# A hybrid encoder layer: half of the tokens normed before their transposes, two GLU tiles side by side, the gate tile first, and the first pair's weight sums on VectorE

## The chip, the cores and the metric

The kernel runs on one core of a Trainium2 chip. The metric is the device time of one execution in microseconds; where runs are repeated, the median is given. All times below are in microseconds unless they are marked as nanoseconds.

The names of the engines in the profile: PE is TensorE (matrix products, and transposes made as products with an identity), PEld its weight loads, DVE is VectorE, ACT is ScalarE, POOL is GpSimd, and SP is SyncE, which issues most of the DMAs. POOL issues those DMAs that add to what lies at their destination.

## The reference

One encoder layer over 1024 tokens of width 1024, all in float32. What is computed, cut to the part that the change touches:

```python
h = _rmsnorm(x, attn_norm_w)                 # x * rsqrt(mean(x*x) + EPS) * w
proj = h @ w_in                              # 1024 -> 8192 columns
glu_in, q, v, z_f, z_b, og, g_a, g_b = split(proj)
a = glu(glu_in)                              # first half * sigmoid(second half), 512 columns
a = dwconv_centred(a, 31 taps) -> layernorm -> silu -> @ pw_w
o = bidirectional HGRN2 scan of q, v, z_f, z_b, normed per head and gated by og
x = x + (sigmoid(g_a) * a + sigmoid(g_b) * o @ o_w) @ w_out
x = x + conv-gated feed-forward of rmsnorm(x)     # d_ff = 2816
return _rmsnorm(x, final_norm_w)
```

## The kernel before, in words

Activations are held transposed: a tile has 128 features on the partitions and 512 tokens along the row, so 1024 tokens are two halves and 1024 features are eight k tiles. Float32 products are made of three products with rounded operands: each operand is split into a high part (a cast on ScalarE, line 121) and a low part (source minus high part, line 118, on VectorE or GpSimd), and `mm3` (lines 143 to 145) issues high x high, high x low and low x high. One output tile of 128 columns for one half of the tokens is 8 k tiles x 3 = 24 products in one PSUM bank.

The order of TensorE's instructions is the order of the program text; the other engines' orders are made by a planner, which takes the text's order as priority and starts ahead of its turn what its cost model holds to be ready. Each engine then works strictly in its own order.

`Stream` and `run_jobs` interleave: a job is a preparation (load the raw weights into a "wr" buffer, of which there are two; split them into two "wp" pages, of which there are four) and a run that yields after every two k tiles (six products, a piece). `s_glu.fill(n)` puts n pieces into the text. When a job starts, the preparation of the next one is put into the text.

The stages around the change:

1. `load_x(0)` issues the loads of the first four tiles of x (128 tokens each), then `load_vectors` issues ten small loads of norm weights, biases and taps; `s_glu.fill()` issues the loads of the first two GLU weight tiles, and `load_x(1)` the other four tiles of x.
2. `input_norm(0)` handles the first half: ScalarE sums the squares of each token tile (line 436), TensorE transposes x itself, six of the eight k tiles ahead; GpSimd raises the mean to the power -1/2 (lines 404 and 405); `spread` brings this row statistic across the partitions with four scaled identities on ScalarE (line 411), a product with ones and a copy (lines 412 and 413). Then for each k tile VectorE multiplies the bank by the norm weight and by the spread statistic (line 455) into an "ev" page, ScalarE makes the high and GpSimd the low part, ScalarE copies the bare transposed x (line 457), and the normed tile and the copy are stored to `d_h` and `d_xt`.
3. The eight GLU column tiles (value j, then gate j, for j from 0 to 3) are made for the first half of the tokens, then again for the second half: 16 jobs of 24 products, 64 pieces. The value's bank is held until the gate's sigmoid (line 493) is there; VectorE's product (line 494) then frees both. `input_norm(1)` runs between these pieces, two pieces for each step.
4. `h_combos` (lines 292 and 508) loads normed tiles back from `d_h` and makes the sums of activations that Strassen's scheme needs; line 532 makes one more set. The remaining GLU pieces run beside it and `s_glu.drain()` ends the GLU.
5. `pair_job` makes two column tiles for both halves by seven instead of eight products of blocks (12 x 7 products, in the order 1, 2, 6, 7, 5, 4, 3). Its preparation needs sums of weight blocks, made by DMAs that add (line 238): `col += src1` from HBM, then the two halves of `rows` in turn. 17 such pairs follow, and the steps of the depthwise conv on VectorE (lines 642 and 645) are put between their pieces.

Behind this come the layer norm and pointwise product of the conv branch, the scans, and the rest of the layer. `x2_evac` loads `d_xt` back there for the residual sum.

The lines that set the pace in the text:

```python
s_glu = Stream(run_jobs([*glu_jobs(0), *glu_jobs(1)], prime=2))
norm0, norm1 = input_norm(0), input_norm(1)
next(norm0)
s_glu.fill()
load_x(1)
turn_vectors()
for _ in norm0:
    pass
s_glu.fill(GLU_FIRST)          # 4
for _ in norm1:
    s_glu.fill(GLU_FILL)       # 2
s_glu.fill(GLU_MORE)           # 16
```

## Time and profile before

| what | value |
|---|---|
| median of 3 runs | 1885.06 us (1883.33 to 1894.11) |
| the profiled execution | 1885.96 us |
| its span | 1884.2 us, 23705 instructions |
| granted TensorE clock, mean | 0.983 |
| ScalarE begins on the first x tile, on the fourth | 4.08 us, 8.70 us |
| first GLU product on TensorE | 21.60 us |
| first product of the first pair | 135.37 us |
| last product of the sixth set of the first pair | 160.22 us |
| last step of the depthwise conv on VectorE | 349.4 us |

How to read it. A row of the timeline has the start, the duration, the engine, the line of the kernel, the operation, its output and inputs by tile name, the shape, and in brackets how long the engine had stood idle and what released it. A row of a table by stretches has the stretch and its length, then the busy time and number of instructions of each engine, the granted TensorE clock (1.00 is full speed), the share of time in which the 16 DMA engines were busy, and what they moved. A row of the waits has who waited for whom, the total, how often, and the longest. Matrix products are pipelined: each is shown some 0.39 us long, but their starts are what counts.

### The profile page before, as it was taken

How to read it: one execution, taken by the hardware profiler on the slowest of the kernel's cores; microseconds unless marked ns; L12 is line 12 of the kernel's file. 1: busy time of each engine (PE TensorE's matmuls, PEld its weight loads, DVE VectorE, ACT ScalarE, POOL GpSimd, SP SyncE). 2: the span in 40 equal slices, each digit the busy share in tenths (PEclk: the TensorE clock that was granted, in tenths of full speed). 3: DMA queues.
4: the chain of work that ended last, by engine and by line, in shares of the span. 5: the costliest groups of instructions: out<-in, count | busy, mean ns of one | idle time of the engine just before them, and what ended most of it. 6: DMA issues, size and time to landing. Idle time of an engine off the chain costs nothing.

```text
span 1884.2 us, 23705 instructions
## 1 busy us (share of the span) xinstructions
PE 1790.5 (95%) x8543; PEld 1478.6 (78%) x8543; DVE 1270.1 (67%) x1860; ACT 797.2 (42%) x1488; POOL 198.0 (11%) x202
## 2 busy tenths in 40 slices
PE   6988999999999999999989999899999999999996
PEld 4767877877787888888878778688888788788885
DVE  3488999635459999989935556676666767534445
ACT  6333343324554655555442144543443434522124
POOL 3101112213100000000000000111111111000000
PEclk9999999999999999999999999999999999999998
DMA  7747788876572333322228666777676766633134
GB/s 264 222 116 165 181 183 204 188 177 156 176 224 79 118 96 117 109 91 93 84 90 240 194 193 185 165 164 145 145 160 147 154 140 129 216 97 94 55 92 162
DMA packets 322764, 282.99 MB, mean 150 GB/s; under 512 B 14798, under 2 KB 244950, under 8 KB 322646
## 3 DMA queue, kind: packets, MB, share of 16 engines
q1 hardware_dynamic: 270854, 240.57, 41.2%
q0 software_dynamic: 51792, 40.90, 15.6%
q8 instruction: 67, 1.10, 0.2%
q14 instruction: 51, 0.42, 0.1%
HBM read 189.14 MB, written 71.83 MB: 139 GB/s over the span
## 4 chain that ended last, share of the span: by engine, by line
PE 48%; DVE 21%; DMA 18%; ACT 6%; issue 4%; POOL 2%; SPq 0%; ACTq 0%; DVEq 0%; POOLq 0%
PE mm L143 12%; PE mm L144 12%; PE mm L145 12%; DMA wr<-wr 3%; DMA tm<-d_a 3%; DVE wp L118 2%; DMA wr<-sw 2%; PE sc L143 2%; PE sc L145 2%; PE sc L144 2%; DVE kG L730 2%; DMA sw<-in_w_in_dram 2%; DVE acc L645 2%; DMA wr<-in_w_in_dram 2%; DVE qF L730 2%
## 5 line engine op out<-in xcount | busy, mean ns | idle before, releaser
L143 PE MATMUL mm<-hx,wp 128*128 128x512 f32 x1176 | 481.4, 409 | 19.4 <-ACT su L266 5.1
L145 PE MATMUL mm<-hx,wp 128*128 128x512 f32 x1176 | 467.2, 397 | 4.3 <-DVE wp L118 4.3
L144 PE MATMUL mm<-hx,wp 128*128 128x512 f32 x1176 | 466.1, 396 | 2.4 <-POOL hx L118 2.4
L121 ACT CAST wp<-wr 128x1024 fp32r<-128x1024 f32 (+2 forms) x196 | 179.7, 917 | 341.8 <-PE mm L144 207.9
L118 DVE TENSOR_TENSOR wp<-wr,wp 128x1024 fp32r<-128x1024 f32 (+2 forms) x196 | 207.2, 1057 | 118.7 <-ACT wp L121 113.0
L143 PEld LDWEIGHTS mm<-hx,wp 128*128 128x128 f32 x1176 | 225.7, 192 | 69.5 <-ACT su L266 7.2
L145 PEld LDWEIGHTS mm<-hx,wp 128*128 128x128 f32 x1176 | 224.8, 191 | 55.6 <-DVE wp L118 6.7
L144 PEld LDWEIGHTS mm<-hx,wp 128*128 128x128 f32 x1176 | 225.6, 192 | 47.9 <-POOL hx L118 4.7
L645 DVE SCALAR_TENSOR_TENSOR acc<-gl,v_b,acc 128x1024 f32<-128x1024 f32 x120 | 149.3, 1279 | 0.5
L1259 DVE TENSOR_TENSOR xr<-mm,xr 128x512 f32<-128x512 f32 x48 | 33.2, 691 | 80.9 <-PE mm L145 80.9
L238 POOL DMA_DIRECT2D wr<-sw x39 | 34.6, 888 | 491.1 <-DVE wp L118 227.6
L838 PE MATMUL sc<-qF,A 128*128 128x128 f32 x512 | 68.8, 277 | 13.8 <-DVE qF L730 13.2
L838 PEld LDWEIGHTS sc<-qF,A 128*128 128x128 f32 x512 | 64.3, 192 | 21.1 <-issue 17.0
L121 ACT CAST wq<-sw 128x1024 fp32r<-128x1024 f32 x39 | 41.0, 1052 | 78.2 <-PE mm L144 68.5
L835 ACT COPY A<-kG 128x512 f32<-128x512 f32 x64 | 39.6, 618 | 73.3 <-DVE kG L730 50.8
L143 PE MATMUL mm<-hy,wp 128*128 128x512 f32 x156 | 62.3, 399 | 6.7 <-ACT wp L121 5.2
L1181 DVE SCALAR_TENSOR_TENSOR tm<-gp,v_a,tm 128x512 f32<-128x512 f32 x88 | 65.7, 748 | 2.3 <-ACT tm L1177 1.1
L266 ACT COPY su<-mm 128x512 f32<-128x512 f32 x78 | 45.3, 581 | 49.9 <-PE mm L145 49.7
L144 PE MATMUL mm<-hy,wp 128*128 128x512 f32 x156 | 62.1, 398 | 0.0
L145 PE MATMUL mm<-hy,wp 128*128 128x512 f32 x156 | 61.7, 396 | 0.0
L143 PE MATMUL sc<-hy,wq 128*128 128x512 f32 x156 | 61.3, 393 | 0.0
L143 PE MATMUL tr<-hx,wp 128*128 128x512 f32 x156 | 61.3, 393 | 0.0
(289 smaller groups left out, 3587.7 us busy)
## 6 DMA issues: line engine op xcount, KB each, us to landing
wr<-in_w_in_dram SPq DMA_DIRECT2D x55, 512.0 KB, 5.3
sw<-in_ffn_w_up_dram SPq DMA_DIRECT2D x44, 256.0 KB, 3.6
sw<-in_ffn_w_up_dram POOLq DMA_DIRECT2D x22, 512.0 KB, 8.9
wr<-in_ffn_w_up_dram SPq DMA_DIRECT2D x22, 512.0 KB, 5.2
d_g<-ft SPq DMA_DIRECT2D x44, 256.0 KB, 5.6
ev<-d_g SPq DMA_DIRECT2D x44, 256.0 KB, 2.8
wr<-sw POOLq DMA_DIRECT2D x39, 256.0 KB, 3.3
wr<-wr POOLq DMA_DIRECT2D x39, 256.0 KB, 4.4
```

The costliest lines, as they stand in the source:

```text
L118: eng.tensor_tensor(lo, src, hi.bitcast(F32), op=ALU.subtract)
L121: A.copy(hi, src)
L143: T.matmul(acc, whi[:, k, :], ahi, start=first, stop=False, skip_group_check=again)
L144: T.matmul(acc, whi[:, k, :], alo, start=False, stop=False, skip_group_check=again)
L145: T.matmul(acc, wlo[:, k, :], ahi, start=False, stop=last, skip_group_check=again)
L238: G.dma_start(o, a, accum_op=ALU.add)
L266: A.copy(t, acc)
L645: V.scalar_tensor_tensor(acc, g[:, k : k + S], tap(k), acc, op0=ALU.mult, op1=ALU.add)
L730: V.tensor_tensor(o, a, b, op=op)
L835: A.copy(A_t.rearrange("p (b x e) -> p b x e", x=2, e=h), pairs(kG, h))
L838: T.matmul(b[:, c * P : (c + 1) * P].rearrange("p (b x e) -> p b x e", x=2, e=h), A_t[:, c * P : (c + 1) * P], view(qF, c * P, [[2 * h, P ...
L1181: V.scalar_tensor_tensor(c, g[:, o + k : o + k + H], vec("fdw", k * NF + j), c, op0=ALU.mult, op1=ALU.add,)
```

## The change

It rewrites the prologue up to the first pair:

- The first half of the tokens is normed before its transposes. `first_norm` multiplies each token tile, 128 tokens on the partitions, by its own statistic (a scalar for each partition; VectorE, 128x1024), and TensorE transposes the result. So `spread` is not called for this half. From the bank ScalarE makes the high part with the norm weight as scale, VectorE the low part straight from the bank, and ScalarE a plain copy for the store to `d_h`. The bare x, which the residual sum needs, is transposed on its own, in eight groups of four transposes (`residual`), copied by VectorE and stored to `d_x0`, a layout in which four k tiles of one token tile lie together; `x2_evac` loads it back in pieces of 128 tokens.
- Only the norm weight's vector is loaded at the beginning; the other nine small loads and their transposes come after `second_norm` (which is the former `input_norm(1)`).
- The first two GLU tiles, gate 0 and value 0, run side by side: for each k tile three products of each (`glu_first`). The next three raw weight tiles are loaded early.
- The gate tile comes ahead of the value tile everywhere: its sigmoid goes into a "tm" page (`gate`), its bank is free then, and the value's product takes the page. The third tile is made for both halves at once; tiles 0, 1 and 2 of the second half follow, and the conv begins with tile 3.
- The first pair's weight sums are made by VectorE (`first=True`), with the second block's raw weights loaded into the second "wr" buffer, and its preparation is put into the text after 17 pieces beside `h_combos`, before the GLU ends. The other pairs keep the DMAs that add.

The diff, cut to its core (`store`, `todo` and `in_pair` are only moved up, and `in_pair` passes `first=n == 0`):

```diff
...
-GLU_MORE = 16
+GLU_MORE = 4
+GLU_LATE = 17
...
-    def pair_job(src0, src1, nk, acts, wpool, pool, evac, su=4):
+    def pair_job(src0, src1, nk, acts, wpool, pool, evac, su=4, first=False):
...
             def add(o, a):
-                G.dma_start(o, a, accum_op=ALU.add)
+                if first:
+                    V.tensor_tensor(o, o, a, op=ALU.add)
+                else:
+                    G.dma_start(o, a, accum_op=ALU.add)
 
...
-            add(col, src1)
+            add(col, raw_w(src1, 2 * nk) if first else src1)
...
@@ -337,12 +341,13 @@
         rows_in.append((v, r, n))
         return v
 
-    def turn_vectors():
-        b = bank("ob")
+    def turn_vectors(tag="ob"):
+        b = bank(tag)
         for i, (v, r, n) in enumerate(rows_in):
             T.transpose(b[:, i * P : i * P + n], r[:n, :], ident[:n, :n])
         for i, (v, r, n) in enumerate(rows_in):
             V.tensor_copy(v, b[:, i * P : i * P + n])
+        rows_in.clear()
...
-    v_a = load_vectors(
-        "v_a",
-        [
-            ("attn", rview(attn_norm_w), ND),
+    vecs = {"v_n": load_vectors("v_n", [("attn", rview(attn_norm_w), ND)])}
+    others = {
+        "v_a": [
...
-    )
-    v_b = load_vectors("v_b", [("cdw", rview(conv_dw_w), CK * NCW)])
-    v_c = load_vectors("v_c", [("fdb", rview(ffn_dw_b), NF)])
-    vecs = {"v_a": v_a, "v_b": v_b, "v_c": v_c}
+        "v_b": [("cdw", rview(conv_dw_w), CK * NCW)],
+        "v_c": [("fdb", rview(ffn_dw_b), NF)],
+    }
...
-    d_xt = scratch("d_xt", ND, 2)
+    d_x0 = dp.tile([P, 4, ND, P], F32, name="d_x0")
+    d_xt = [[d_x0[:, :, k, :], scratch(f"d_xt_{k}")] for k in range(ND)]
...
-    tags0 = iter(["sc", "tr", "sc", "tr", "mm", "mm", "sc", "tr"])
-
-    def input_norm(half):
-        xs = x_in[half * 4 : half * 4 + 4]
+    def first_norm():
+
+
+        xs = x_in[:4]
         ss = cp.tile([P, 4], F32, name=nm("ss"), tag="ss", bufs=2)
+        rs = cp.tile([P, 4], F32, name=nm("rs4"), tag="rs4", bufs=1)
+        xn = []
         for i, xt in enumerate(xs):
-            junk = p0.tile([P, D], F32, tag="junk", name=nm("junk"), bufs=2)
+            t = p0.tile([P, D], F32, tag="xn", name=nm("xn"), bufs=4)
+            A.activation(t, xt, AF.Square, accum_out=ss[:, i : i + 1])
+            rstd_small(rs[:, i : i + 1], ss[:, i : i + 1], D)
+            V.tensor_scalar(t, xt, rs[:, i : i + 1], None, op0=ALU.mult)
+            xn.append(t)
+
+        def residual(i, g, tag):
+            b = bank(tag)
+            for k in range(4):
+                T.transpose(
+                    b[:, k * P : (k + 1) * P], xs[i][:, (4 * g + k) * P : (4 * g + k + 1) * P], ident
+                )
+            t = page(p0, "xr", 7)
+            V.tensor_copy(t, b)
+            nc.sync.dma_start(
+                d_x0[:, i, 4 * g : 4 * g + 4, :], t.rearrange("p (k t) -> p k t", k=4)
+            )
+
+        def turn(b, i, k):
+            T.transpose(b[:, i * P : (i + 1) * P], xn[i][:, k * P : (k + 1) * P], ident)
+
+        residual(0, 0, "mm")
+        residual(0, 1, "mm")
+        turn_vectors("mm")
+        banks = [bank(t) for t in ("sc", "tr", "sc", "tr", "ob")]
+        for i in range(4):
+            for k, b in enumerate(banks):
+                turn(b, i, k)
+        yield
+        late = {2: (1, 0, "mm"), 3: (1, 1, "tr"), 4: (2, 0, "ob")}
+        late |= {5: (2, 1, "sc"), 6: (3, 0, "tr"), 7: (3, 1, "sc")}
+        for k in range(ND):
+            b, g = banks[k], vec("attn", k)
+            hi, lo, raw = hx(), hx(), page(p0, "raw", ND)
+            A.activation(hi, b, AF.Copy, scale=g)
+            V.scalar_tensor_tensor(lo, b, g, hi.bitcast(F32), op0=ALU.mult, op1=ALU.subtract)
+            A.activation(raw, b, AF.Copy, scale=g)
+            nc.sync.dma_start(d_h[k][0], raw)
+            ht[1 if k < NK2 else 2].append((hi, lo))
+            yield
+            if k + 5 < ND:
+                b = bank(("sc", "tr", "sc")[k])
+                for i in range(4):
+                    turn(b, i, k + 5)
+                banks.append(b)
+            if k in late:
+                residual(*late[k])
+
+    def second_norm():
+        xs = x_in[4:]
+        ss = cp.tile([P, 4], F32, name=nm("ss"), tag="ss", bufs=2)
+        junk = p0.tile([P, D], F32, tag="xn", name=nm("junk"), bufs=4)
+        for i, xt in enumerate(xs):
             A.activation(junk, xt, AF.Square, accum_out=ss[:, i : i + 1])
         banks = []
 
         def turn(k):
-            b = bank(next(tags0) if half == 0 else "tr")
+            b = bank("tr")
             for i in range(4):
                 T.transpose(b[:, i * P : (i + 1) * P], xs[i][:, k * P : (k + 1) * P], ident)
             banks.append(b)
 
-        ahead = 6 if half == 0 else 1
-        for k in range(ahead):
-            turn(k)
+        turn(0)
         yield
         rstd_small(ss, ss, D)
-        rs = spread(ss, bank("ob"), page(p0, "rs", 2))
+        rs = spread(ss, bank("ob"), page(p0, "rs", 1))
         yield
         for k in range(ND):
             b = banks[k]
@@ -455,13 +511,11 @@
             V.scalar_tensor_tensor(raw, b, vec("attn", k), rs, op0=ALU.mult, op1=ALU.mult)
             hl = split(hx(), hx(), raw, G)
             A.copy(xt, b)
-            if k + ahead < ND:
-                turn(k + ahead)
-            nc.sync.dma_start(d_h[k][half], raw)
-            nc.sync.dma_start(d_xt[k][half], xt)
-            if half == 0:
-                ht[1 if k < NK2 else 2].append(hl)
-            elif k < NK2:
+            if k + 1 < ND:
+                turn(k + 1)
+            nc.sync.dma_start(d_h[k][1], raw)
+            nc.sync.dma_start(d_xt[k][1], xt)
+            if k < NK2:
                 h12.append(hl)
             else:
                 ht[3].append(hl)
@@ -480,23 +534,117 @@
         G.memset(g[:, PAD + S :], 0.0)
         gl.append(g)
 
-    held = {}
-
-    def glu_jobs(half):
-        for j in range(NCW):
-
-            def evac_a(hf, acc):
-                held[0] = acc
-
-            def evac_b(hf, acc, j=j):
-                sg = tmp()
-                A.activation(sg, acc, AF.Sigmoid)
-                V.tensor_tensor(
-                    gl[j][:, PAD + hf * H : PAD + (hf + 1) * H], held[0], sg, op=ALU.mult
-                )
-
-            yield std_job(in_cols(j * P), ND, h_std, evac_a, (half,))
-            yield std_job(in_cols(CW + j * P), ND, h_std, evac_b, (half,))
...
+    gate = {}
+    early = []
+
+    def evac_b(j):
+        def evac(hf, acc):
+            gate[j, hf] = tmp()
+            A.activation(gate[j, hf], acc, AF.Sigmoid)
+
+        return evac
+
+    def evac_a(j):
+        def evac(hf, acc):
+            V.tensor_tensor(
+                gl[j][:, PAD + hf * H : PAD + (hf + 1) * H], acc, gate.pop((j, hf)), op=ALU.mult
+            )
+
+        return evac
+
+    def glu_tiles(j, halves):
+        yield std_job(in_cols(CW + j * P), ND, h_std, evac_b(j), halves)
+        yield std_job(in_cols(j * P), ND, h_std, evac_a(j), halves)
+
+    def glu_first():
+
+
+        def prep():
+            ws = []
+            for c in (CW, 0):
+                raw = raw_w(in_cols(c), ND)
+                ws.append(split(w_page(ND), w_page(ND), raw, V))
+            return ws
+
+        def run(ws):
+            accs = [bank("mm"), bank("mm")]
+            for k in range(ND):
+                for acc, w in zip(accs, ws):
+                    mm3(acc, w, h_std(k, 0), k, k == 0, k == ND - 1)
+                yield
+            evac_b(0)(0, accs[0])
+            evac_a(0)(0, accs[1])
+
+        return prep, run
+
+    def glu_jobs():
+        def loaded(job, key, pages):
+            def prep():
+                return split(pages(), pages(), early[key], V)
+
+            return prep, job[1]
+
+        def early_page():
+            return p0.tile([P, ND, P], F32R, tag="xn", name=nm("wp"), bufs=4)
+
+        yield glu_first()
+        job0, job1 = glu_tiles(1, (0,))
+        yield loaded(job0, 0, early_page)
+        yield loaded(job1, 1, lambda: w_page(ND))
+        job0, job1 = glu_tiles(2, (0,))
+        yield loaded(job0, 2, lambda: w_page(ND))
+        yield job1
+        yield from glu_tiles(3, (0, 1))
+        for j in (0, 1, 2):
+            yield from glu_tiles(j, (1,))
 
     def h_combos():
         def hy():
@@ -508,21 +656,29 @@
                 nc.sync.dma_start(t, d_h[kk][half])
             combos(ht, k, b11, b12, b22, hy)
 
-    s_glu = Stream(run_jobs([*glu_jobs(0), *glu_jobs(1)], prime=2))
-    norm0, norm1 = input_norm(0), input_norm(1)
-    next(norm0)
+    s_glu = Stream(run_jobs(glu_jobs(), prime=1))
     s_glu.fill()
+    ahead = p0.tile([P, ND, P], F32, name="ahead")
+    nc.sync.dma_start(ahead, in_cols(CW + P))
     load_x(1)
+    early += [ahead, raw_w(in_cols(P), ND), raw_w(in_cols(CW + 2 * P), ND)]
+    for n, _ in enumerate(first_norm()):
+        if n > 0:
+            s_glu.fill()
+    s_glu.fill(GLU_FIRST)
+    for _ in second_norm():
+        s_glu.fill(GLU_FILL)
+    for name, parts in others.items():
+        vecs[name] = load_vectors(name, parts)
+    s_glu.fill(GLU_FIRST)
     turn_vectors()
-    for _ in norm0:
-        pass
-    s_glu.fill(GLU_FIRST)
-    for _ in norm1:
-        s_glu.fill(GLU_FILL)
     s_glu.fill(GLU_MORE)
     p0.release()
     p1 = tc.alloc_tile_pool(name="p1", bufs=1, reuse_waits="tile")
     h_combos()
+    s_glu.fill(GLU_LATE)
+    pair0 = in_pair(0)
+    w_pair0 = pair0[0]()
     s_glu.drain()
     h12.clear()
     for k in range(NK2):
@@ -533,7 +689,7 @@
         ht[4].append(split(hx(), hx(), b21, V))
 
 
-    lbl = v_a[:, vec_off["lb"][1] : vec_off["lb"][1] + 2 * NH]
+    lbl = vecs["v_a"][:, vec_off["lb"][1] : vec_off["lb"][1] + 2 * NH]
...
-    jobs = collections.deque(in_pair(n) for n in range(NPAIRS))
+    jobs = collections.deque(in_pair(n) for n in range(1, NPAIRS))
+    jobs.appendleft((lambda: w_pair0, pair0[1]))
     s_pairs = Stream(run_jobs(jobs, 4))
 
     def conv_steps():
-        for j in range(NCW):
+        for j in (3, 0, 1, 2):
             acc = p1.tile([P, S], F32, tag="ca", name=nm("acc"), bufs=2)
             g = gl[j]
 
@@ -1102,7 +1212,8 @@
 
         def evac(half, acc):
             xt = ev()
-            nc.sync.dma_start(xt, d_xt[i][half])
+            to = xt if half else xt.rearrange("p (c t) -> p c t", c=4)
+            nc.sync.dma_start(to, d_xt[i][half])
             t = page(p4, "x2", 2)
             V.tensor_tensor(t, acc, xt, op=ALU.add)
             nc.sync.dma_start(d_x2[i][half], t)
```

129 lines of the change are left out of this document (65 added, 64 removed).

## The prediction, made before the change was run

> **What bounds the kernel now.** I read the page first, then the stretches of the beginning, then the TensorE rows of the timeline, and last the waits. TensorE carries the span:
>
> ```profile
> PE 1790.5 (95%) x8543; PEld 1478.6 (78%) x8543; DVE 1270.1 (67%) x1860; ACT 797.2 (42%) x1488; POOL 198.0 (11%) x202
> ```
>
> So a change to the prologue is worth the TensorE time that it saves there, as long as nothing behind it becomes the bound. The busy times by stretch (columns: PE, PEld, DVE, ACT, POOL busy, granted clock, DMA share, GB/s):
>
> ```profile
> 0.00:21.60 21.60, 8.78 (x38) 6.63 (x38) 6.03 (x15) 13.88 (x25) 5.24 (x21) 0.95 0.77 274
> 21.60:33.40 11.80, 9.37 (x29) 5.76 (x28) 3.75 (x5) 9.69 (x21) 8.70 (x9) 0.80 0.87 310
> 33.40:81.20 47.80, 47.80 (x225) 39.11 (x223) 16.71 (x19) 19.30 (x29) 13.32 (x9) 1.00 0.83 237
> 81.20:160.40 79.20, 65.57 (x242) 50.87 (x240) 64.41 (x89) 28.17 (x39) 5.58 (x7) 0.87 0.49 126
> 160.40:340.00 179.60, 175.84 (x769) 143.71 (x769) 174.18 (x165) 67.95 (x96) 32.16 (x28) 1.00 0.82 185
> ```
>
> From 33.4 to 81.2 nothing is to be had: TensorE is full at full clock. The loss lies before 33.4 and between 81.2 and 160.4. In the TensorE rows the first product of the GLU starts at 21.60, its 24 products end with a group of four transposes at 33.11, and the next job starts at 33.46:
>
> ```profile
> 21.60 0.78 PE L143 MATMUL mm<-hx,wp 128*128 128x512 f32 x1
> ...
> 33.11 0.60 PE L442 MATMUL tr<-ident,xt 128*128 128x128 f32 x4
> 33.46 0.48 PE L143 MATMUL mm<-hx,wp 128*128 128x512 f32 x1
> ...
> 80.95 0.39 PE L144 MATMUL mm<-hx,wp 128*128 128x512 f32 x1
> 81.18 0.39 PE L145 MATMUL mm<-hx,wp 128*128 128x512 f32 x1
> ```
>
> Dense products start 0.23 apart (the last two rows), and a group of four transposes moves what follows by 0.35 (33.11 to 33.46). So the first job's 24 products, worth 24 x 0.23 = 5.5, took 33.46 - 21.60 = 11.9, of which 0.35 is transposes: 6.0 are lost, to slow products (granted clock 0.80 in that stretch) and to waits for the h tiles. Four more stretches lose time, at a granted clock of 0.66 to 0.77:
>
> ```profile
> 81.20:91.20 10.00, 7.05 (x18) 4.99 (x17) 7.95 (x11) 5.60 (x8) 0.00 (x0) 0.66 0.42 132
> 98.60:105.00 6.40, 3.91 (x10) 2.96 (x10) 3.54 (x5) 2.58 (x4) 0.00 (x0) 0.73 0.77 236
> 114.70:122.00 7.30, 4.41 (x13) 3.40 (x13) 7.30 (x11) 0.60 (x1) 0.00 (x0) 0.77 0.25 72
> 140.80:152.70 11.90, 6.62 (x15) 4.63 (x15) 7.86 (x15) 4.41 (x5) 2.38 (x3) 0.71 0.82 165
> ```
>
> With 18, 10, 13 and 15 products of 0.23 they lose 10.0 - 4.1 = 5.9, 6.4 - 2.3 = 4.1, 7.3 - 3.0 = 4.3 and 11.9 - 3.4 = 8.5. The first three (14.3 together) lie in the GLU, the last in the first Strassen pair. What ended the waits, first for 62 to 122, then for 122 to 165 (total, times, longest):
>
> ```profile
> ACT wq L121 <- DMA sw<-in_w_in_dram: 9.6, 1, 9.6
> ...
> DVE tm L292 <- DMA su<-d_h: 6.6, 3, 5.2
> ...
> PE mm L145 <- DVE wp L118: 3.7, 2, 2.9
> ...
> PE mm L143 <- ACT tm L493: 2.5, 1, 2.5
> ```
>
> ```profile
> ACT wp L121 <- DMA wr<-wr: 6.2, 1, 6.2
> ...
> PE mm L143 <- ACT wp L121: 5.2, 1, 5.2
> ```
>
> ScalarE, in order, stood 9.6 on a weight sum that GpSimd's accumulating DMA was still making; behind it stood the sigmoid and the cast that TensorE needed at 81.2. The gap at 98.6 is a PSUM bank that a late sigmoid held; the gap at 114.7 a weight split queued behind combinations that had waited for loads of d_h; the gap at 140.8 the chain of accumulating DMAs for the first pair.
>
> **The change part by part.** Durations are from the profiled execution, 1885.96 with a span of 1884.2, which is 0.9 above the median of 1885.06; what I work out is a difference, and I take it from the median.
>
> *The start.* These rows price it:
>
> ```profile
> 8.70 1.06 ACT L436 ACTIVATE junk<-xt 128x1024 f32<-128x1024 f32 x1
> ...
> 14.64 1.04 ACT L121 CAST wp<-wr 128x1024 fp32r<-128x1024 f32 x1
> ...
> 17.63 0.62 ACT L121 CAST hx<-ev 128x512 fp32r<-128x512 f32 x1 [0.21 <-DVE ev L455]
> ```
>
> ```profile
> 10.22 1.04 POOL L405 TENSOR_TENSOR ss<-ss,mhalf 128x4 f32<-128x4 f32 x1
> ...
> 26.25 6.24 POOL L118 TENSOR_TENSOR hx<-ev,hx 128x512 fp32r<-128x512 f32 x5
> ```
>
> ```profile
> 15.71 1.23 DVE L118 TENSOR_TENSOR wp<-wr,wp 128x1024 fp32r<-128x1024 f32 x1
> 16.86 0.75 DVE L455 SCALAR_TENSOR_TENSOR ev<-sc,v_a,rs 128x512 f32<-128x512 f32 x1
> ```
>
> ```profile
> 119.99 0.81 DVE L642 TENSOR_SCALAR acc<-gl,v_b,v_a 128x1024 f32<-128x1024 f32 x1
> ```
>
> ```profile
> 9.72 1.03 SPq L130 DMA_DIRECT2D wr<-in_w_in_dram x2
> ```
>
> ```profile
> 11.49 1.66 PE L442 MATMUL mm<-ident,xt 128*128 128x128 f32 x8
> ```
>
> The fourth token tile's sum of squares starts at 8.70 and its power ends on GpSimd at 11.26 either way. Then one VectorE multiply of 128x1024 (0.81, as L642) makes the last normed tile at 12.1, five transposes of 0.21 (1.66 / 8) end at 13.2, ScalarE's high part (0.62) at 13.9, VectorE's low part (0.75) at 14.6. Gone from this path are the diagonal, the ones-matmul and its copy. The weights no longer stand on SP behind ten small vector loads: the two loads go out with the x tiles instead of at 9.72, and at the 310 GB/s of the 21.6 to 33.4 row each 512 KB takes 1.7 behind the x tiles that land at 8.7, so 10.4 and 12.1. Two casts (1.04) and two splits (1.23) interleave with the above; VectorE's sum behind the last normed tile is 1.23 + 1.23 + 0.75, which gives 15.3 for the low part. Between 13.9 and 18 (weights late, ScalarE's order unlucky) I take 15.0: 6.6 saved, bounds 3.6 and 7.7.
>
> *Two tiles side by side.* Each h tile then feeds six products, 6 x 0.23 = 1.4, against ScalarE's two instructions (2 x 0.62 = 1.24) and VectorE's 0.75 plus a residual copy (at most 0.75) for each: TensorE is the longer one, where before GpSimd's low part was (6.24 / 5 = 1.25 each) against 3 x 0.23 = 0.7 of products. The start at low clock falls away if the transposes run on into the products. Of the 6.0 lost I give 4.0 back, bounds 0 and 6.0; what may remain is ScalarE serving squares of the second half and casts in between.
>
> *Added on TensorE.* Eight groups of transposes for the residual, six of them behind the first product, and three of the normed groups that used to lie ahead of it: 9 x 0.35 = 3.2. The three transposes of the other vectors move into the dense part: at most another group, 0.35. The eight residual stores replace eight others of the same size; loading them back in pieces of 512 bytes lies 1000 us later on prefetched buffers, cost nothing. The nine vector loads now stand on SP after the second norm and need three of the four "tm" buffers; eight pieces of products (48 x 0.23 = 11.0) cover them. The third tile's second half follows the second norm's last tile closely: 1.0, bounds 0 and 3.
>
> *Gate ahead of value.* The gate's bank is freed by its sigmoid alone and the value's by the product, so a late sigmoid has two jobs (2 x 5.5) of slack rather than one. This removes the 98.6 gap. The pair's preparation, placed behind 17 pieces and without a DMA sum in front of ScalarE's cast, removes most of the 81.2 gap. The combinations and their waits for d_h (6.6) stay, with 24 pieces (24 x 1.4 = 33) still to come in program order; one gap like that of 114.7 is likely to stay, elsewhere. Of 14.3 I give 10.0 back, bounds 0 and 14.3.
>
> A rule for what such a gap costs: after 98.6 TensorE waited 2.5 and ran the next products at a granted clock of 0.73 over 6.4. [...]
>
> *First pair's sums on VectorE.* Adds of 128x1024 (1.23) and twice 128x512 (at most 0.75 each) replace the accumulating DMAs whose last wait was 6.2. They need both weight buffers, which come free as the last two GLU splits end, some 1.5 jobs (8) before the pair; product 6, the first that needs the sums and the third in order, starts 2 x 12 x 0.23 = 5.5 after the pair. Behind VectorE's wait for the load stand the conv's steps, which nobody awaits then. Of 8.5 I give 6.5 back, bounds 0 and 8.5.
>
> *Knock-on.* VectorE gains 4 x 0.81 + 8 x 0.75 + 2.7 = 11.9, in the prologue where it has room (6.03 + 3.75 + 16.71 busy up to 81.2), but from 160.4 to 340 it is 97% busy. Evacuations late by conv steps: 1.5, bounds 0 and 11.9. Sigmoid and Exp tables may be swapped once more on ScalarE, hidden at 28.17 of 79.2 busy.
>
> Sum: 6.6 + 4.0 + 10.0 + 6.5 = 27.1 saved; 3.2 + 0.4 + 1.0 + 1.5 = 6.1 spent; 21.0 net. 1885.1 - 21.0 = 1864.
>
> **The rivals.** *The waits move.* The d_h loads and in-order ScalarE make new gaps of 2 to 3, each followed by slow products. Only 2, 4 and 2 of the three lost sums come back: 6.6 + 8 - 6.1 = 8.5, 1877. For it: three different causes made the three gaps. Chance 0.22.
>
> *Nearly clean.* 7 + 5.5 + 13 + 8 - 4.5 = 29, 1856. [...] Chance 0.18.
>
> *The pair's preparation still blocks.* VectorE is given the add for the pair ahead of a GLU split, and stands on the load as ScalarE did for 9.6. Neither GLU gaps nor pair come back: 6.6 + 4 - 6.1 = 4.5, 1881. Here the change does not do what it says. Chance 0.09.
>
> *VectorE sets the pace (slower).* If conv and pairs up to 340 are bound by VectorE (5.4 idle in 179.6) and not by TensorE (3.8 idle), the saving is eaten there and the 11.9 of new work comes on top: 1897. It decides once the waits of TensorE for VectorE's evacuations between 160 and 340 exceed 21. Against it: the conv's steps run ahead of need, so they can be late. Chance 0.06.
>
> **How the numbers follow.** My forecast, 1864 with its own range of 1858 to 1871, has 0.45. Faster or slower by over 1% means below 1866 or above 1904, about what a measurement of this kernel can tell from no change. Below 1866 lie the clean case (0.18) and some 0.7 of the forecast's (0.32): 0.50. Above 1904 only a VectorE case worse than bounded: 0.05. The rest is 0.45. The bounds of the terms reach from 1885 - (7.7 + 6.0 + 14.3 + 8.5 - 3.7) = 1852 to 1885; leaving out 1 in 10 on each side gives 1854 to 1881.
>
> **What would show it.** First product near 15 and the granted clock near 1.0 up to 33; two "mm" accumulators filled in turn; TensorE without idle up to the second norm's end; the last GLU product near 119 and no wait for a "wr<-wr" DMA in the first pair; the pair's sixth set of products, whose last ends the 160.4 stretch, done near 138. The prediction is wrong if the granted clock still falls below 0.8 in several stretches before 140, or if TensorE's waits for VectorE between 140 and 320 come to more than 10.

## The result and the profile after

| | before | after |
|---|---|---|
| median, beside each other on one chip | 1883.28 us | 1865.28 us |
| range of the runs | 1879.50 to 1894.11 | 1861.64 to 1873.64 |
| ratio of the runs | | 0.9916, 95% interval 0.9898 to 0.9935 |
| profiled execution, its span | 1885.96, 1884.2 | 1873.26, 1871.5 |

The change is faster by 0.8%: by the interval 12 to 19 us, where 21.0 were forecast. The profiled execution of the changed kernel stands near the upper end of its range, 12.7 ahead of the one before.

To see where the time was won, I follow TensorE's order of work, which is the same behind the GLU in both kernels, and note when it reaches the same four products: the first of the GLU, the last of pair 0's sixth set (the end of the 160.4 stretch in the prediction), the first of pair 1's second set, and one in the conv's layer norm, behind fourteen more pairs. The last adds up the squares for the variance (line 420 before, line 424 in the changed kernel); the expectations below call it the mean's product, and so do I, though the product for the mean itself stands 11 ahead of it (429.31 and 415.77). TensorE has the same 1166 products from pair 1 to it in every kernel below. In the timeline of the kernel before (start, duration, then what ended a wait) the last three are:

```profile
160.22 0.39 PE L145 MATMUL sc<-hx,wq 128*128 128x512 f32 x1
...
166.26 0.39 PE L143 MATMUL tr<-hx,wp 128*128 128x512 f32 x1
...
440.84 0.49 PE L420 MATMUL ob<-ones_m,tm 128*128 128x1 f32 x3 [2.32 <-POOL tm L659]
```

and in the changed kernel, with its three largest stops in between:

```profile
15.58 0.50 PE L144 MATMUL mm<-hx,wp 128*128 128x512 f32 x1 [1.36 <-ACT hx L475]
...
101.45 0.50 PE L144 MATMUL mm<-hx,wp 128*128 128x512 f32 x1 [2.86 <-ACT tm L591]
...
120.51 0.50 PE L146 MATMUL mm<-hx,wp 128*128 128x512 f32 x1 [0.92 <-DVE wp L119]
...
137.05 0.39 PE L146 MATMUL sc<-hx,wq 128*128 128x512 f32 x1
...
139.56 0.50 PE L144 MATMUL mm<-hx,wp 128*128 128x512 f32 x1 [2.12 <-DVE ev L541]
...
146.76 0.39 PE L144 MATMUL tr<-hx,wp 128*128 128x512 f32 x1
...
427.02 0.38 PE L424 MATMUL ob<-ones_m,tm 128*128 128x1 f32 x2 [2.06 <-POOL tm L769]
```

The lead over the kernel before is thus 6.0 at the first product, 23.2 at the sixth set, 19.5 at pair 1, 13.8 at the mean, and 12.7 at the end. So the prologue won what it was to win, and then two fifths went again: 3.7 between the sixth set and pair 1, 5.7 over the pairs beside the conv. (The stop at 139.56 is in front of pair 0's seventh set, which is the last of the pair.) The stretches of the changed kernel (columns as in the prediction):

```profile
15.58:33.40 17.82, 17.32 (x86) 14.15 (x87) 10.52 (x16) 15.53 (x26) 1.21 (x2) 0.90 0.87 316
...
76.00:98.60 22.60, 22.59 (x101) 18.22 (x98) 21.26 (x36) 10.78 (x16) 0.00 (x0) 1.00 0.59 176
98.60:105.00 6.40, 3.55 (x16) 2.94 (x17) 5.90 (x9) 4.59 (x7) 0.00 (x0) 1.00 0.74 230
...
122.00:137.40 15.40, 14.95 (x65) 11.75 (x63) 15.40 (x29) 7.45 (x10) 2.78 (x2) 1.00 0.74 164
137.40:146.80 9.40, 7.28 (x26) 5.79 (x26) 8.32 (x11) 3.40 (x5) 2.44 (x2) 0.82 0.71 198
146.80:427.00 280.20, 270.58 (x1167) 220.30 (x1165) 214.10 (x208) 96.97 (x136) 53.92 (x47) 0.99 0.80 180
```

TensorE is full from 76 to 98.6, where the kernel before lost 5.9 at 81.2; one stop of 2.9 is left in the GLU, at 98.6, and pair 0 runs nearly full. The loss shows in the last two rows. From pair 1 to the mean TensorE needs 280.2, where the kernel before needed 440.84 - 166.26 = 274.6 for the same products. What TensorE waited for in those stretches, first before, then after (total, times, longest):

```profile
PE mm L143 <- DVE ev L588: 3.5, 2, 1.8
PE mm L143 <- ACT su L266: 1.5, 2, 0.7
```

```profile
PE mm L144 <- DVE ev L541: 4.6, 6, 2.0
PE mm L144 <- ACT su L270: 2.9, 2, 2.1
```

Both are copies of a finished quadrant out of PSUM, by VectorE and by ScalarE, that came late.

### The profile page after: what moved, and what is told of

Read it like the earlier page. It is cut to its first block, busy times and chain, and to the rows that moved or that the text cites. A ratio compares the mean times of both kernels' runs of the same rounds, so it can differ in the third digit from the quotient of the medians.

```text
span 1871.5 us, 23768 instructions
## 1 busy us (share of the span) xinstructions
PE 1788.6 (96%) x8574; PEld 1481.4 (79%) x8574; DVE 1275.7 (68%) x1874; ACT 796.2 (43%) x1483; POOL 185.8 (10%) x197
## 4 chain that ended last, share of the span: by engine, by line
PE 45%; DVE 23%; DMA 18%; ACT 6%; issue 5%; POOL 1%; SPq 0%; ACTq 0%; POOLq 0%; DVEq 0%
PE mm L144 12%; PE mm L145 12%; PE mm L146 12%; DMA wr<-wr 4%; DVE wp L119 3%; DMA wr<-sw 3%; DMA sw<-in_w_in_dram 3%; DMA tm<-d_a 3%; DVE kG L840 2%; DVE acc L755 2%; PE sc L144 2%; PE sc L146 2%; PE sc L145 2%; DVE qF L840 2%; DVE DE L840 2%
## 5 line engine op out<-in xcount | busy, mean ns | idle before, releaser
L119 DVE TENSOR_TENSOR wp<-wr,wp 128x1024 fp32r<-128x1024 f32 (+2 forms) x193 | 203.4, 1054 | 123.0 <-ACT wp L122 116.2
L948 PE MATMUL sc<-qF,A 128*128 128x128 f32 x512 | 69.8, 280 | 13.3 <-DVE qF L840 13.1
```

Source lines behind the costliest of these rows:

```text
L119: eng.tensor_tensor(lo, src, hi.bitcast(F32), op=ALU.subtract)
L948: T.matmul(b[:, c * P : (c + 1) * P].rearrange("p (b x e) -> p b x e", x=2, e=h), A_t[:, c * P : (c + 1) * P], view(qF, c * P, [[2 * h, P ...
```

## The experiments

The theory was that the gain has three separable sources (start, GLU order, pair 0's preparation), and that it is given back because VectorE, which is full up to 340 and got more to do, evacuates late. The rivals: that the gain has one source, and that VectorE is only the last in a chain that starts with the loads. The table has the four products again for every kernel, each from one profile, and the medians; the kernel before ran beside each group with a median of 1880.65 to 1883.28.

| kernel | first product | sixth set | pair 1 | mean | median us | ratio to before |
|---|---|---|---|---|---|---|
| before | 21.60 | 160.2 | 166.3 | 440.8 | | 1 |
| changed | 15.58 | 137.1 | 146.8 | 427.0 | 1865.28 | 0.9916 [0.9898, 0.9935] |
| changed, again | 15.54 | 137.7 | 147.4 | 427.8 | 1864.84 | 0.9921 [0.9894, 0.9948] |
| pair 0 by DMA | 15.63 | 141.2 | 146.8 | 431.4 | 1870.05 | 0.9931 [0.9906, 0.9957] |
| one tile after the other | 17.43 (a transpose) | 139.4 | 149.0 | 432.5 | 1862.80 | 0.9907 [0.9894, 0.9920] |
| normed behind the transposes | 18.48 | 139.5 | 149.2 | 426.1 | 1861.16 | 0.9903 [0.9889, 0.9916] |
| no exponential | 15.68 | 136.9 | 142.6 | 428.1 | 1867.73 | 0.9924 [0.9897, 0.9951] |
| no residual transposes | 13.58 | 133.1 | 142.8 | 418.2 | 1861.49, one run | |
| value first | 15.53 | 145.5 | 151.8 | 432.0 | 1870.36 | 0.9952 [0.9933, 0.9972] |
| early pair 0 alone, on before | 21.26 | 143.6 | 149.9 | 433.3 | 1873.15 | 0.9965 [0.9946, 0.9983] |
| half the taps | 15.72 | 137.3 | 145.4 | 424.3 | 1861.83 | 0.9908 [0.9881, 0.9936] |
| before, half the taps | 21.31 | 159.6 | 165.6 | 445.2 | 1884.60 | 1.0016 [0.9995, 1.0038] |
| late masks | 15.37 | 136.7 | 146.6 | 420.1 | 1859.84 | 0.9898 [0.9868, 0.9927] |
| late masks, normed behind | 17.96 | 136.5 | 146.2 | 418.8 | 1861.01 | 0.9899 [0.9873, 0.9924] |

The two profiles of the changed kernel agree within 0.8 at each product, so for one program the table tells apart what differs by more than about 1. An edit anywhere can also change the order in which the planner lets the other engines work, so a difference from one profile of each need not be the edit's own doing. The medians of the variants, a few us apart with intervals of 5 to 10 us, mostly do not.

**The changed kernel once more**

> The changed kernel once more. Theory A (the terms of the prediction add up in the prologue, and what is given back behind it is chance, such as late DMAs): median 1865, the sixth product set of the first pair ends at 137 within 1, and the waits that cost time behind it (at 139.6, 259.7 and 369.4 in the profile of the changed kernel) lie elsewhere or are shorter. Rival C (VectorE's new load gives time back in fixed places): the same waits at 139.6, 199.3, 259.7 and 320 come back, each 1 to 2.5.

It has the same stops at 101.45 and 140.18 and the same lead, 22.6 at the sixth set and 13.1 at the mean. Of the later waits that the expectation names, those at 259.7 and 369.4 come back (2.8 and 1.9, at 259.99 and 370.95), those at 199.3 and 320 do not, so theory and rival were half right each. But its span is 1857.9, not 1871.5. The 13.6 between these two executions of one program lie wholly behind the mean, which they reach at 427.0 and 427.8. That part of the kernel is untouched by the change, and its time varies by itself, as the last section shows: this sets how far the medians can be trusted here.

**Pair 0's sums by DMA again**, at the new early place:

```
-            first=n == 0,
+            first=False,
```

> The changed kernel, but the first pair's weight sums made by accumulating DMAs again, its preparation at the same place in the text. Theory A: the first pair's term alone comes back, 6.5 slower than the changed kernel, with a wait of about 5 for a wr<-wr DMA in the first pair and the GLU ahead of it as without gaps as before. Rival B (one cause, the DMA sum that blocks ScalarE, made nearly all of the loss of the kernel before, in the GLU too): ScalarE stands on the sum again, the GLU has its gap back, 12 to 20 slower.

TensorE in that kernel, and ScalarE's longest wait from 120 to 142:

```profile
128.88 0.79 PE L144 MATMUL mm<-hy,wp 128*128 128x512 f32 x1 [4.64 <-ACT su L270]
```

```profile
ACT wp L122 <- DMA wr<-wr: 7.2, 1, 7.2
```

The wait for the sums stays, as forecast: ScalarE stands 7.2 on a cast whose sum is still being made, the copy of a quadrant that comes behind it in its order is late, and TensorE stops 4.6. VectorE's sums save 3.5 to 4.1 at the sixth set. But at pair 1 both kernels stand at 146.8: the stop at 139.56, which takes all of it in the changed kernel, is not there in this one.

**One tile after the other** at the start, the first two value and gate tiles as separate jobs:

```
-        yield glu_first()
+        yield from glu_tiles(0, (0,))
...
-    s_glu = Stream(run_jobs(glu_jobs(), prime=1))
+    s_glu = Stream(run_jobs(collections.deque(glu_jobs()), prime=2))
...
-        if n > 0:
+        if n > 0 and n % 2 == 0:
             s_glu.fill()
+    s_glu.fill(4)
```

> The changed kernel, but gate 0 and value 0 of the first half one after the other instead of side by side. Theory A: 4 slower, since TensorE then has 0.7 of products for each h tile that ScalarE takes 1.3 to make; bounds 1 and 6. Rival B: within 1 of the changed kernel.

```profile
17.43 0.48 PE L460 MATMUL sc<-ident,xn 128*128 128x128 f32 x1 [3.82 <-ACT raw L477]
```

The sixth set is 1.7 to 2.3 later, so side by side is worth that there, though not for the reason expected. The stop of 3.8 lies ahead of the first product: a piece is two h tiles here, so a group of normed transposes stands in front of it, and waits for ScalarE's copy of the tile whose bank it takes. From the first product at 18.20 to 33.40 TensorE does not wait at all (busy for 15.20 of 15.20, at a clock of 0.83), although each h tile feeds three products.

**The first half normed behind its transposes**, as before, with everything else of the change:

```
-            V.tensor_scalar(t, xt, rs[:, i : i + 1], None, op0=ALU.mult)
...
+            V.scalar_tensor_tensor(raw, b, vec("attn", k), rs, op0=ALU.mult, op1=ALU.mult)
+            hl = split(hx(), hx(), raw, G)
+            A.copy(xt, b)
...
-            if k in late:
-                residual(*late[k])
```

> The changed kernel, but the first half normed behind its transposes again (spread, the low part on GpSimd, the bare x copied from the bank by ScalarE), so without the eight residual groups; everything else stays. Theory A, by rows: the diagonal (1.28), the ones-matmul (1.10), the copy (0.58) and the multiply (0.75) replace 0.81 + 1.05 + a second pass, so the first product comes about 1 later (16.6), GpSimd's 1.25 for each h tile stays under 6 products of 0.23, and six residual groups (2.1) fall away: within 2 of the changed kernel, on either side. Rival D (norming ahead of the transposes is what makes the start): first product at 18 or later and 4 to 6 slower.

```profile
18.48 0.80 PE L144 MATMUL mm<-hx,wp 128*128 128x512 f32 x1 [2.14 <-ACT hx L122]
```

and in the kernel before, TensorE ahead of its first product at 21.60:

```profile
18.79 0.66 PE L442 MATMUL sc<-ident,xt 128*128 128x128 f32 x4 [3.42 <-ACT tm L457]
20.83 1.12 PE L442 MATMUL tr<-ident,xt 128*128 128x128 f32 x4 [1.38 <-ACT tm L457]
```

The first product of the GLU starts 2.9 later than in the changed kernel, as the rival had it, so half of the 6.0 won at the start comes from norming ahead. The other half is the order of TensorE's work, and not the weights that stood behind ten small loads: in the kernel before the first normed tile is as early as here (VectorE's multiply at 16.86 and 17.00) and its high part follows at 17.63, but two more groups of transposes stand in front of the first product and wait for ScalarE's copies of the banks that they take. In the changed kernel, and in this one, the first products come ahead of these groups. By the sixth set 1.9 to 2.5 of it is left (the residual transposes are gone as well), and at the mean nothing: 426.1 against 427.0 and 427.8. The median, 1861.16, is not above that of the changed kernel. Norming ahead, the longest part of the diff, buys nothing that lasts, by this profile.

**No exponential.** The kernel computes x + 1 in place of the small exponential for the bounds of the heads:

```
-    A.activation(lbw[:, 1, :], lbw[:, 0, :], AF.Exp)
+    V.tensor_scalar(lbw[:, 1, :], lbw[:, 0, :], 1.0, None, op0=ALU.add)
```

> The changed kernel, but the one Exp of the lower bounds, which for a single layer is of zero, replaced by a VectorE addition of one, so that ScalarE keeps the sigmoid's table through the GLU. Theory E (the wait at 101.45 is in part the table load of 1.28 in front of the sigmoid that TensorE waited 2.9 for): that wait falls to 1.6 or less and the pair's sixth set ends 1 to 3 earlier than 137; no second Sigmoid table load at 99.5. Theory A: the same gap is left by the combinations' loads, nothing changes within 0.5.

```profile
100.92 0.50 PE L144 MATMUL mm<-hx,wp 128*128 128x512 f32 x1 [1.45 <-ACT tm L591]
...
159.49 0.50 PE L144 MATMUL mm<-hx,wp 128*128 128x512 f32 x1 [3.12 <-DVE ev L541]
```

and ScalarE in the changed kernel, ahead of the sigmoid at 100.80:

```profile
99.50 1.28 ACT L591 ACT_TABLE_LOAD   x1
```

The stop before 101 falls from 2.86 to 1.45, so half of it was this table load of 1.28, which the exponential forces on the sigmoid behind it; the kernel without the exponential has none there. The sixth set is no earlier, though. That kernel comes to the stop 0.9 behind the changed one, which it had lost by 21.6, so it leaves it only 0.5 ahead; and the stops at 113.5 and 120.4, for a weight split on VectorE, take most of that: 0.1 of lead is left at the sixth set. That was my theory's miss. What I did not expect is pair 1, 4.2 earlier. VectorE in this kernel:

```profile
134.71 1.27 DVE L755 SCALAR_TENSOR_TENSOR acc<-gl,v_b,acc 128x1024 f32<-128x1024 f32 x1
...
136.18 0.67 DVE L541 TENSOR_TENSOR ev<-su,mm 128x512 f32<-128x512 f32 x1
...
136.98 1.21 DVE L119 TENSOR_TENSOR wq<-sw,wq 128x1024 fp32r<-128x1024 f32 x1
```

and in the changed kernel:

```profile
136.29 1.27 DVE L755 SCALAR_TENSOR_TENSOR acc<-gl,v_b,acc 128x1024 f32<-128x1024 f32 x1
...
137.69 1.21 DVE L119 TENSOR_TENSOR wq<-sw,wq 128x1024 fp32r<-128x1024 f32 x1
138.83 0.67 DVE L541 TENSOR_TENSOR ev<-su,mm 128x512 f32<-128x512 f32 x1
```

The evacuation ev<-su,mm, which has to read the bank before pair 0's seventh set adds to it, runs at 136.18 in the one; in the other VectorE's program has one more conv step and the split for a later pair in front of it, and it runs at 138.83. That order is the stop at 139.56, with the slow products behind it (a granted clock of 0.50 from 140.69 to 144.10). At the mean the 4.2 are gone (428.1), and the first of it goes one pair later, to the same order. VectorE without the exponential, ahead of the stop at 159.49:

```profile
157.62 1.22 DVE L119 TENSOR_TENSOR wq<-sw,wq 128x1024 fp32r<-128x1024 f32 x1
158.75 0.68 DVE L541 TENSOR_TENSOR ev<-su,mm 128x512 f32<-128x512 f32 x1
```

**No residual transposes.** The residual's transposes of the first half are left out, and it is stored untransposed:

```
-            b = bank(tag)
-            for k in range(4):
-                T.transpose(
...
-            V.tensor_copy(t, b)
+            V.tensor_copy(t, xs[i][:, 4 * g * P : (4 * g + 4) * P])
```

> The changed kernel, but x is stored for the residual without its transposes (a plain copy on VectorE stands in for them), so the residual is that of another layout. Theory A: six groups of 0.35 come off TensorE behind the first product, the pair's sixth set ends 2.1 earlier, at 135. Rival: the residual groups fill waits for the h tiles, within 0.5 of 137.

The sixth set ends 4.0 to 4.6 earlier. Of that 0.9 is won at the start: the first product stands at 13.58, but the second waits for VectorE's low part until 15.66 (16.59 in the changed kernel). The rest are the six groups behind the first product. In the changed kernel two of them lie like this:

```profile
27.19 0.60 PE L450 MATMUL ob<-ident,xt 128*128 128x128 f32 x4
...
29.02 0.60 PE L450 MATMUL sc<-ident,xt 128*128 128x128 f32 x4
```

Six products of 0.23 stand between them, so a group takes 29.02 - 27.19 - 1.38 = 0.45, six of them 2.7. The two together are 3.6; where the other 0.4 to 1.0 comes from is open. This is the price of norming ahead.

**Value tile ahead of gate tile**, everything else as changed:

```
     def glu_tiles(j, halves):
-        yield std_job(in_cols(CW + j * P), ND, h_std, evac_b(j), halves)
         yield std_job(in_cols(j * P), ND, h_std, evac_a(j), halves)
+        yield std_job(in_cols(CW + j * P), ND, h_std, evac_b(j), halves)
```

> The changed kernel, but the value tile ahead of the gate tile again, its bank held until the gate's sigmoid is there. Theory A: the slack of a late sigmoid is one job instead of two, new gaps between 60 and 120 of 2 to 5 together and their slow clock, the pair's sixth set at 140 to 144. Rival: with the DMA sum gone from ScalarE's way the sigmoid is never that late, within 1 of 137.

```profile
96.75 0.80 PE L144 MATMUL mm<-hx,wp 128*128 128x512 f32 x1 [8.62 <-ACT tm L591]
```

With both accumulators held until the sigmoid, a late sigmoid (at 96.10) costs 8.6 in one stop, not 2.9; the sixth set is 7.9 to 8.5 later, more than expected, and the mean's product 4.2 to 4.9. Gate first is worth that.

**The early pair 0 alone**, on the kernel before: the loads and sums of pair 0 behind 17 pieces of the GLU and by VectorE, nothing else changed:

```
     h_combos()
+    s_glu.fill(17)
+    pair0 = in_pair(0)
+    w_pair0 = pair0[0]()
     s_glu.drain()
...
+                if first:
+                    V.tensor_tensor(o, o, a, op=ALU.add)
```

> The kernel before with one part of the change: the first pair's sums on VectorE and its preparation put into the text 17 pieces after the combinations begin. Theory A: the first product stays at 21.6 and the first job's 6.0 stay lost, the gap at 81.2 (5.9) and the pair's (6.5) come back, the bank gap at 98.6 stays: 10 to 12 off, the pair's sixth set at 149. Rival B (that DMA sum made nearly all of the loss): sixth set at 142 or earlier.

```profile
96.55 0.50 PE L143 MATMUL mm<-hx,wp 128*128 128x512 f32 x1 [4.18 <-ACT tm L544]
```

This alone ends the sixth set 16.6 earlier than the kernel before, and it removes two of the three large stops in the GLU, those at 81.2 and 114.7: only the one in front of the sigmoid, at 96.55, is left. Of the 16.6, 7.5 are left at the mean and about as much in the median (1873.15 for 1880.65). The sixth set at 143.6 is nearer to the rival's 142 than to my 149, which was too late by 5, because I had put these GLU stops down to the order of gate and value and to the combinations. The terms overlap: 16.6 here and 8 for gate first are together more than the 14.3 + 8.5 that there were to win less what stays.

**Half of the conv's taps.** Every second tap of the conv is left out, in the changed kernel and in the kernel before, which takes 60 of 120 operations of 1.28 from VectorE up to 340:

```
-                V.scalar_tensor_tensor(
-                    acc, g[:, k : k + S], tap(k), acc, op0=ALU.mult, op1=ALU.add
-                )
+                if k % 2 == 0:
+                    V.scalar_tensor_tensor(
+                        acc, g[:, k : k + S], tap(k), acc, op0=ALU.mult, op1=ALU.add
+                    )
                 yield
```

> The changed kernel with every odd conv tap left out (60 VectorE operations of 128x1024, 72 us; the conv's output is not the reference's). Read from the first product of pair 1 to the product for the mean behind the conv: 280 in the changed kernel, 274.5 in the one before; the mean's product stands at 427 and 441. Theory (what the prologue won is lost again because VectorE, full until 340, evacuates late): with VectorE relieved this interval falls to 267 to 270 and the wait at 139.6 goes, so the mean's product starts at 409 to 414. Rival (the loads or ScalarE hold the pairs back, VectorE is only named last): the interval stays at 277 to 281 and the mean's product at 422 or later. The tail behind the mean should be the same for both.

> The kernel before with the same odd conv taps left out (the conv's output is not the reference's). Theory: it had only 7.7 of waits in the interval, which fall away, 267 to 270; the mean's product starts near 434, and so the lead of the change there is the whole of what the prologue won, 20 to 24, where it is 13.5 with all taps. Rival: the interval stays near 274 and the lead near 13.5.

In the changed kernel with half the taps, first TensorE's waits from pair 1 to the mean, then a stretch of the pairs (columns as above), then one of TensorE's stops with what ScalarE and VectorE did ahead of it, in the timeline:

```profile
PE mm L144 <- ACT su L270: 7.6, 7, 2.5
PE mm L144 <- DVE ev L541: 2.6, 1, 2.6
```

```profile
146.80:340.00 193.20, 185.35 (x811) 151.45 (x810) 114.02 (x113) 69.02 (x97) 34.76 (x31) 1.00 0.80 183
```

```profile
228.09 1.04 ACT L122 CAST wp<-wr 128x1024 fp32r<-128x1024 f32 x1 [5.56 <-DMA wr<-wr]
...
229.17 1.23 DVE L119 TENSOR_TENSOR wp<-wr,wp 128x1024 fp32r<-128x1024 f32 x1 [4.23 <-ACT wp L122]
...
229.53 0.58 ACT L270 COPY su<-mm 128x512 f32<-128x512 f32 x1
...
230.16 0.50 PE L144 MATMUL mm<-hy,wp 128*128 128x512 f32 x1 [2.49 <-ACT su L270]
```

and its other large stop, with VectorE ahead of it:

```profile
159.87 1.22 DVE L119 TENSOR_TENSOR wq<-sw,wq 128x1024 fp32r<-128x1024 f32 x1
161.01 0.68 DVE L541 TENSOR_TENSOR ev<-su,mm 128x512 f32<-128x512 f32 x1
...
161.74 0.50 PE L144 MATMUL mm<-hx,wp 128*128 128x512 f32 x1 [2.58 <-DVE ev L541]
```

The theory falls, as far as it goes by VectorE's load. With VectorE busy for 114 of 193 the stretch from pair 1 to the mean still takes 424.3 - 145.4 = 278.9 (280.2 with all taps, 267 to 270 expected), and in the kernel before it even takes 445.2 - 165.6 = 279.6 (274.6 with all taps). The lead of the changed kernel at the mean is 20.9 with half the taps, as the theory had it, but only because the kernel before became slower by 5.0 in the pairs with less to do. The waits add up to 10.2, not less than the 7.5 of the changed kernel. For the stop at 230.16 the rows show why: VectorE had been idle for 4.2; it waited for ScalarE's cast, ScalarE had waited 5.6 for a sum of weights by accumulating DMA, and the copy that frees TensorE's bank stood behind that cast. That chain is the wait of pair 0 again, in the pairs that still sum by DMA. The stop at 161.74 is of the other kind, and so is one at 139.81 of 2.1: VectorE works there without a pause, and conv steps and a split for the next pair stand ahead of the evacuation in its order, as in the changed kernel at 139.56. Half of the steps are gone, but the order is not. So it is not how much VectorE has to do, but at some stops a chain that begins elsewhere, and at others what stands ahead in VectorE's order.

**Masks and the exponential behind the conv**, where VectorE is not full: the chain of the lbw rows and build_masks() are moved, as they are, behind

```
     for _ in conv_steps():
         s_pairs.fill(CONV_FILL)
+    lbl = vecs["v_a"][:, vec_off["lb"][1] : vec_off["lb"][1] + 2 * NH]
...
+    build_masks()
```

> The changed kernel with the masks and the small exponential chain built behind the conv instead of ahead of it, where VectorE is not full. Theory (VectorE's burst at pair 0 and the second table load cost the stops at 101.4 and 139.6): pair 0's sixth set ends 1 to 2 earlier than 137.0, pair 1's first product starts at 141 to 143 rather than 146.8, the mean's product at 420 to 424, the time some 4 under the changed kernel's. Rival (the wait only moves, as when the exponential alone was taken out: pair 1 at 142.6 but the mean's product at 428): the mean's product at 426 to 429 and the time as the changed kernel's within 2.

```profile
139.39 0.50 PE L144 MATMUL mm<-hx,wp 128*128 128x512 f32 x1 [2.35 <-DVE ev L541]
...
420.10 0.38 PE L424 MATMUL ob<-ones_m,tm 128*128 128x1 f32 x2 [1.30 <-POOL tm L769]
```

```profile
PE mm L144 <- DVE ev L541: 3.0, 3, 1.4
PE mm L144 <- ACT su L270: 1.6, 3, 0.7
```

The number at the mean came as the theory had it (420.1, expected 420 to 424), but not by its way: the stop at 139.39 is still there, since conv steps and the split still stand ahead of the evacuation, and pair 1 is no earlier (146.6, expected 141 to 143). It is the stretch from pair 1 to the mean that is shorter, 273.5 with waits of 4.6. So 7 of the 9 that were given back are won again; why the pairs run smoother with the masks out of the way is open: VectorE's load is not the reason by the runs with half the taps, a changed order of its work may be.

**The same, and normed behind the transposes:**

> As the kernel with the late masks, and the first half normed behind its transposes as before, so that the nine groups of residual transposes go. Theory: the late masks' gain on top of the spread kernel's 426.1 at the mean's product: 419 to 423, and a time of 1855 to 1860. Rival (waits only move): 425 to 428, and 1860 to 1866.

The mean's product starts at 418.8, within the theory's 419 to 423 but for 0.2, while the median, 1861.01, lies in the rival's 1860 to 1866 and not in the theory's 1855 to 1860. Both versions with late masks have the lowest ratios of all, 0.990, but their intervals overlap that of the change (0.9898 to 0.9935): the profiles show 7 to 9 less up to the mean, the times do not resolve it.

## Why the prediction was right, and where not

The time (1865.3 for 1864) and the sign came out, though the saving is 18.0 and not 21.0: the forecast started from 1885.06, and the kernel before ran at 1883.28 beside the change. The sum of the prologue did too: 23.2 and 22.6 at the sixth set, where the terms without the knock-on gave 27.1 - 4.6 = 22.5. By its steps:

- **The start**: 6.0 of 6.6, first product at 15.58 (15.0 forecast). The last step was not a weight cast but VectorE, which copied the vector's rows at 14.58 behind two residual copies and a split. Only half of it is due to norming ahead. The reason given for the rest, the weights behind ten small loads, was wrong: it is the two groups of transposes that waited ahead of the first product, a wait for which the prediction had no term.
- **Two tiles side by side**: 1.7 to 2.3 of 4.0. The granted clock in the first stretch is 0.90, not near 1.0: TensorE waits 1.4 at the first product and the clock falls once, to 0.50 from 17.8 to 21.2. That TensorE would run out of h tiles with one tile after the other did not show: it stopped ahead of its first product, and not behind it up to 33.4.
- **Added on TensorE**: the residual's six groups behind the first product were forecast at 6 x 0.35 = 2.1; the residual costs 4.0 to 4.6. A group takes 0.45, and the two ahead of the first product delay the start by 0.9.
- **GLU gaps and first pair**, 10.0 and 6.5: together about right, wrongly divided. Early preparation of pair 0 alone gives 16.6; gate first 8, in which it overlaps. That the gap at 114.7 came from the combinations' waits for d_h failed as a step: in that kernel these waits stay (4.8 in all for 6.6) and the gap goes. The left-over gap was forecast "elsewhere", and gate first was to remove the one at 98.6; it is that one which is left. Half of it is the swap of tables (a load of 1.28 at 99.50), which the prediction had put at nothing, "hidden".
- **Knock-on**: the step that failed. It was put at 1.5 (bounds 0 to 11.9), and measured 9.4: 3.7 behind the sixth set, from an evacuation that stands behind conv steps and a split in VectorE's order, and 5.7 from pair 1 to the mean. That evacuations come late behind conv steps was the right kind of cause for the first; that the amount of work on VectorE sets the cost was not, by the runs with half the taps. The 5.7 rest on one profile of the kernel before, and half the taps alone lengthened that stretch by 5.0 there, so how much of them is the change's own is open.

That 1865 lies so near to 1864 with 9.4 in place of 1.5 has a second reason. The lead at the mean is 13.1 to 13.8, the medians differ by 18.0 (12 to 19 by the interval). Behind the mean the two profiles of the changed kernel differ by 14 with one program, so some us of the agreement are chance. The range was also too narrow for its own terms: their bounds reach up to 1885.1 - 3.6 + (3.2 + 0.4 + 3 + 11.9) = 1900, not 1885.

Of the rivals, "the waits move" happened in part, one stage later than it said: not in the GLU but behind it. "VectorE sets the pace" did not: TensorE's waits for VectorE between 140 and 320 are 6.3, under the 10 at which I would have called the prediction wrong. Nor did the clock fall in several stretches before 140: it did so, to 0.50, once in the first profile (17.8) and twice in the second (17.6 and 102.95).

What stays open: what sets the pairs' pace up to the mean. For the stop at 230.16 the chain back to a DMA's sum is shown, and for those at 139.56, 159.49 and 161.74 the order of VectorE's work; that these sums cause all of the 273 to 285 that the variants need for the same products is only argued. Sums by VectorE in all pairs, which would tell, were not tried.

## What to carry to other kernels

When several stops lie ahead of the same shared work, try that work alone first: preparing one pair earlier, with its sums on VectorE, gave 16.6 of 23.2 in the prologue (7.5 of 13.8 at the mean), while the longest part of the diff gave nothing that lasted. Follow a gain by the start of the same instruction in both traces, stage by stage; here 23 shrank to 14 within 300 us, which neither the total nor the busy shares would have told. And do not blame the engine that a wait names: take load from it, see whether the wait goes, and read what stands ahead of the awaited operation in that engine's order.

## What the runs showed of the hardware

The same stop was followed by two different clocks. The changed kernel and its second profile both stop for 2.86 and restart at 101.45; the one keeps the full clock, the other runs at half from 102.95 on. Stretches around the restart, first of the changed kernel, then of its second profile:

```profile
99.72:103.14 3.42, 1.69 (x7) 1.43 (x8) 2.92 (x4) 1.74 (x3) 0.00 (x0) 1.00 0.80 271
103.14:106.55 3.41, 3.41 (x16) 2.81 (x15) 3.41 (x6) 2.27 (x4) 0.47 (x2) 1.00 0.71 190
```

```profile
99.53:102.95 3.42, 1.50 (x7) 1.24 (x7) 2.90 (x4) 1.86 (x2) 0.00 (x0) 1.00 0.79 270
102.95:106.36 3.41, 3.41 (x10) 2.64 (x9) 3.41 (x7) 2.34 (x4) 0.29 (x2) 0.50 0.66 180
```

Behind the stop the first has 16 products in 3.41 at a clock of 1.00, the second 10 at 0.50, and the product at 107.03 in the first starts 1.6 later in the second. So the stop of 2.86 cost its wait alone in the one, and 1.6 more in the other. A shorter one was followed by half clock too: behind the stop of 2.1 that ends at 139.56 in the changed kernel the clock is 0.50 from 140.69 to 144.10, which is the 0.82 of the row from 137.4 to 146.8. Up to the mean three more stretches of that profile run at 0.50, from 17.8, 260.1 and 369.4 on, each 3.4 long. What decides whether the clock falls behind a stop is not shown by these runs.

Where the low stretches lie differs from run to run, and so does their number, 12 in the changed kernel's first profile (mean clock 0.984) and 8 in its second (0.992); of the 12 eight last 3.4, three 6.8, and the last, from 1861.0 on, lies behind TensorE's work. From the mean's product to TensorE's last group of transposes (at 1858.72 and 1845.15) it has the same 6826 instructions in both and is busy with them for 1387.8 and 1378.5: of the 14.3 by which the first is slower there, 9.2 are longer busy time, and waits the rest. So the larger part of the 13.6 between their spans is time in which the same work took longer, in the profile with the lower mean clock.
